# Two units for the modulated features, unit columns in the chunk's bank, and later steps around the halves of q, k and v

## The chip, the core and the metric

One core of a Trainium2 chip. The metric is the device time of one execution in microseconds. TensorE (PE) multiplies matrices into PSUM, which has eight banks; VectorE (DVE), ScalarE (ACT) and GpSimd (POOL) do elementwise work; SyncE (SP) issues nearly all DMAs, in the order in which they stand in the program. Each engine works through its own instructions in order and waits on the others by semaphores.

## What is computed

One layer of a hybrid mixer. 128 context tokens and 1024 latent tokens of 1024 features are normalised and modulated, projected by one matrix to q, k, v, an attention gate, an input of a recurrence and its gate; differential attention (8 heads, two softmax maps each) and a bidirectional gated recurrence run side by side, each output is multiplied by its SiLU gate, both go through one output projection, and the result is normalised, gated and added to x.

```python
sh, sc, gt = split(silu(cond) @ w_ada + b_ada)        # per token group
h = rms_norm(x, g_pre) * (1 + sc) + sh
q, k, v, g_att, x_lru, g_lru = split(h @ w_in)
o = softmax(q1 k1) v - lam * softmax(q2 k2) v          # per head, rotary q and k
att = rms_norm(o) * 0.8 * silu(g_att)
u = conv4(x_lru); a, b = gates(u)                      # both directions
lru = (scan(a_f, b_f) + reverse_scan(a_b, b_b)) * silu(g_lru)
y = x + gt * rms_norm(concat(att, lru) @ w_out)
```

Returned are y of both groups, the context's k and v, and the recurrence's final states.

## The kernel before

All 1152 tokens lie along the free axis, features along the partitions: `hTh[k]`, `hTl[k]` are the high and low fp16 halves of slice k (128 of 1024 features) of h. A weight of 48 (`order`, 128 output features each) is loaded as fp32 (`wraw`), its sum of squares taken on ACT (`w_square`, L286), summed over partitions by a matmul with ones (`w_unit`, L292) into one PSUM column, turned into a power of two on DVE (`power_of_two`, L190 to L195), scaled and cast to halves (`w_hi` on ACT, L306; `w_lo` on DVE, L312). `w_back` keeps the inverse of weight unit times feature unit. A projection chunk (`chunk`) is 24 matmuls: 8 slices by three products of halves, for 384 tokens, in one bank. `w_ahead` keeps three to five weights prepared ahead of the chunk in work.

PSUM is two pools: `big` (three banks, one buffer) and `small` (five banks). Chunks, unit columns (`wu`) and the small sums all take `small` buffers; a buffer is given out again in the order of release, and its next writer waits for its last reader.

**Stage 1, to 78 us.** Four parts of the modulation, A and C (scale) and B and D (shift) of the first and second half of the features, are products of `w_ada` (16 loads of 512 KB) with two columns. A, B and C are fp32 matmuls (`mod`, L419, 16 records each); D is summed on DVE (`mod_add`, L430 and L432, into `dsum`) and put across partitions by four matmuls. Squares of x are taken on ACT (`sqsum`), added on DVE (L499), summed by matmuls (`ssq`, L524), the root by `newton`, spread over partitions into `rb` (L530). Then `normed` (x times the root, L476), one unit for all features (`unit_h`), `modulate` on ACT or DVE, `h_lo` on DVE, and the first block's three chunks (x of block 0), slice by slice.

**Stage 2, to 415 us: eight rounds** of the recurrence. Round n: three chunks of the LRU gate (`g`), in rounds 1 to 6 three chunks of an attention gate (`ga` with hTh operands), then the four block gates of round n (`ga` in the `big` buffer, with `uh`, `ul`, `gwh`) with the three chunks of the next block's input (`x`) between them. `silu` (L703, ACT) and `silu_mult` (L709, DVE) read the gate chunks. DVE and ACT do round n-1's decays, weights, scans and mix meanwhile; `conv`, `split_u` make `u`, `uh`, `ul` of round n.

**Stage 3, to 760 us:** q, k chunks (24 matmuls each) and v tiles (24 matmuls of 256 columns), each followed by a `tick()`. `after(d, f)` runs f behind the d-th next tick. Steps of a q or k are `squares` (ACT, L868), `turned` (`power`, a matmul L879 and DVE, then `rope`, DVE), `halves` (ACT L893, DVE L894), `send` (DMA). Of a pair of v: `peak` (transpose L964, DVE), `spread` (L974), `halves` (ACT L983, DVE L984), `send` (L990). The output gate (`gate_step`) is summed on DVE and totalled by matmuls (`gacc`, L1031) of its halves (`ghl`). After the last v pair come two attention-gate blocks (`g_block`), six ticks, and attention's first loads (`load_k`, `load_q`, `load_wo`, `load_lt`) on SP.

**Stage 4:** attention and the output projection.

## Time and profile before

| | |
|---|---|
| median of 3 runs | 1281.56 us (1280.08 to 1284.37) |
| the profiled execution | 1290.48 us |
| its span | 1288.7 us |
| granted TensorE clock, mean | 0.963 of 2.4 GHz |
| TensorE busy | 1149.6 us (89%) |
| DVE busy | 1029.9 us (80%) |
| ACT busy | 781.9 us (61%) |
| POOL busy | 301.2 us (23%) |

The profile comes from one execution; its times are microseconds from the span's start, a mean time of an instruction is given in ns where that is said. A matmul's row shows its latency; matmuls overlap, so the distance of two starts is what one costs. "Idle" in brackets is how long the engine stood before the row, and what it waited for last. Two levels of the clock occur, 1.2 and 2.4 GHz; over a stretch the profile gives the mean as a share of 2.4.

### The profile page before, as it was taken

How to read it: one execution, taken by the hardware profiler on the slowest of the kernel's cores; microseconds unless marked ns; L12 is line 12 of the kernel's file. 1: busy time of each engine (PE TensorE's matmuls, PEld its weight loads, DVE VectorE, ACT ScalarE, POOL GpSimd, SP SyncE). 2: the span in 40 equal slices, each digit the busy share in tenths (PEclk: the TensorE clock that was granted, in tenths of full speed). 3: DMA queues.
4: the chain of work that ended last, by engine and by line, in shares of the span. 5: the costliest groups of instructions: out<-in, count | busy, mean ns of one | idle time of the engine just before them, and what ended most of it. 6: DMA issues, size and time to landing. Idle time of an engine off the chain costs nothing.

```text
span 1288.7 us, 20513 instructions
## 1 busy us (share of the span) xinstructions
PE 1149.6 (89%) x7792; PEld 792.3 (61%) x7792; DVE 1029.9 (80%) x1788; ACT 781.9 (61%) x1283; POOL 301.2 (23%) x172
## 2 busy tenths in 40 slices
PE   6599999999999679989999979988898888999787
PEld 1265655665666556675675847766666665667676
DVE  5886797779779767876867647898898989999877
ACT  4477467557746546544454347777777776777632
POOL 0000000000000000000000013345865576666624
PEclk8799999999999989999999999999999998999999
DMA  9321222231231243643525275899998889799864
GB/s 365 127 66 42 88 77 62 88 113 41 86 99 60 94 126 127 161 126 115 152 88 136 52 249 113 190 204 225 180 233 181 208 212 189 189 210 220 199 204 163
DMA packets 277818, 188.75 MB, mean 146 GB/s; under 512 B 196172, under 2 KB 246092, under 8 KB 276952
## 3 DMA queue, kind: packets, MB, share of 16 engines
q1 hardware_dynamic: 277432, 186.60, 54.4%
q8 instruction: 61, 1.00, 0.3%
q10 hardware_dynamic: 288, 0.85, 0.2%
q14 instruction: 37, 0.30, 0.1%
HBM read 102.20 MB, written 46.94 MB: 116 GB/s over the span
## 4 chain that ended last, share of the span: by engine, by line
PE 40%; DVE 32%; ACT 11%; DMA 7%; issue 6%; POOL 2%; SPq 2%; DVEq 0%; ACTq 0%; POOLq 0%
DVE mx L1195 6%; DVE e L1223 4%; PE ga L119 3%; DMA t<-a 3%; PE ga L120 3%; PE ga L121 2%; PE x L119 2%; PE x L120 2%; PE x L121 2%; PE s L1186 2%; DVE wlo L312 2%; PE s L1188 2%; PE v L119 2%; PE v L120 2%; PE v L121 2%
## 5 line engine op out<-in xcount | busy, mean ns | idle before, releaser
L1205 ACT ACTIVATE e<-s,mx,back 128x1152 f32<-128x1152 f32 (+1 forms) x144 | 175.5, 1219 | 70.7 <-DVE fa L1213 20.3
L1227 POOL TENSOR_TENSOR a<-e,a 128x1152 f16<-128x1152 f32 (+1 forms) x72 | 157.9, 2192 | 172.6 <-ACT a L1226 164.2
L113 POOL TENSOR_TENSOR wol<-wor,woh 128x512 fp32r<-128x512 f32 x24 | 33.5, 1398 | 694.1 <-ACT woh L218 694.0
L1195 DVE TENSOR_REDUCE mx<-s 128x1 f32<-128x1152 f32 (+1 forms) x144 | 177.3, 1232 | 22.7 <-PE s L1188 21.9
L120 PEld LDWEIGHTS <-whi 128*128 128x128 f16 x960 | 95.2, 99 | 82.3 <-issue 26.4
L119 PEld LDWEIGHTS <-whi 128*128 128x128 f16 x960 | 97.5, 102 | 66.3 <-issue 10.5
L121 PEld LDWEIGHTS <-wlo 128*128 128x128 f16 x960 | 95.2, 99 | 66.3 <-issue 5.6
L1186 PE MATMUL s<-kt,qt 128*128 128x384 f16 (+1 forms) x400 | 90.6, 332 | 46.2 <-ACT e L1205 42.9
L1223 DVE SCALAR_TENSOR_TENSOR e<-e,fa,e 128x1152 f32<-128x1152 f32 (+1 forms) x72 | 114.9, 1596 | 6.4
L119 PE MATMUL pv<-vt,t 128*128 128x128 f16 x584 | 104.7, 223 | 6.0 <-DMA t<-a 3.6
L119 PE MATMUL po<-woh,lt 128*128 128x512 f32 x216 | 98.8, 457 | 6.3 <-DVE acc L1152 3.3
L120 PE MATMUL pv<-vt,t 128*128 128x128 f16 x584 | 104.2, 222 | 0.0
L121 PE MATMUL pv<-vt,t 128*128 128x128 f16 x584 | 104.1, 222 | 0.0
L1226 ACT CAST a<-e 128x1152 f16<-128x1152 f32 (+1 forms) x72 | 75.8, 1053 | 40.7 <-DVE e L1223 25.9
L1188 PE MATMUL s<-kt,qt 128*128 128x384 f16 (+1 forms) x400 | 89.9, 331 | 0.0
L121 PE MATMUL po<-woh,lt 128*128 128x512 f32 x216 | 86.2, 399 | 0.0
L120 PE MATMUL po<-wol,lt 128*128 128x512 f32 x216 | 86.0, 398 | 0.0
L119 PE MATMUL v<-whi,hTh 128*128 128x256 f16 x288 | 80.1, 278 | 3.1 <-ACT qfq L735 2.6
L312 DVE SCALAR_TENSOR_TENSOR wlo<-wraw,wunit,whi 128x1024 f16<-128x1024 f32 x48 | 61.5, 1281 | 25.2 <-ACT whi L306 25.2
L120 PE MATMUL v<-wlo,hTh 128*128 128x256 f16 x288 | 80.1, 278 | 1.1 <-DVE wlo L312 1.1
L1186 PEld LDWEIGHTS <-qt 128*128 128x128 f16 x400 | 34.2, 99 | 76.0 <-issue 63.4
L121 PE MATMUL v<-whi,hTl 128*128 128x256 f16 x288 | 80.2, 278 | 0.0
(342 smaller groups left out, 3239.2 us busy)
## 6 DMA issues: line engine op xcount, KB each, us to landing
wraw<-in_w_in_dram SPq DMA_DIRECT2D x48, 512.0 KB, 3.6
lt<-mix SPq DMA_DIRECT2D x27, 512.0 KB, 4.5
qs<-hlq SPq DMA_DIRECT2D x64, 144.0 KB, 3.2
qt<-qs SPq DMA_DIRECT2D x72, 128.0 KB, 3.7
wa<-in_w_ada_dram SPq DMA_DIRECT2D x16, 512.0 KB, 11.0
wor<-in_w_out_dram SPq DMA_DIRECT2D x32, 256.0 KB, 3.3
mix<-amo SPq DMA_DIRECT2D x6, 1152.0 KB, 6.0
vs<-v SPq DMA_DIRECT2D x8, 640.0 KB, 6.3
```

The lines of the kernel that those rows point to most:

```text
L113: eng.tensor_tensor(out=lo, in0=val, in1=f(hi), op=ALU.subtract)
L119: PE.matmul(out, lhsT=lh, rhs=rh, start=start, stop=False)
L120: PE.matmul(out, lhsT=lh, rhs=rl, start=False, stop=False)
L121: PE.matmul(out, lhsT=ll, rhs=rh, start=False, stop=stop)
L312: V.scalar_tensor_tensor(out=lo[:, i % 2], in0=raws[i], scalar=wunit[:, i:i + 1], in1=hi[:, i % 2], op0=ALU.mult, op1=ALU.subtract)
L1186: PE.matmul(sps[:, j, :w_], lhsT=qt[:, mp], rhs=kt_[:, mp, c], start=True, stop=False)
L1188: PE.matmul(sps[:, j, :w_], lhsT=qt[:, 2 + mp], rhs=kt_[:, mp, c], start=False, stop=True)
L1195: V.tensor_reduce(out=d["mx"][:, mp:mp + 1], in_=sv, axis=AX.XY, op=ALU.max, negate=True)
L1205: S.activation(out=e_[:, :nk].rearrange("p (j c) -> p j c", c=w_), in_=sv, func=AF.Exp, bias=d["mx"][:, mp:mp + 1], scale=unit, accum_out= ...
L1223: V.scalar_tensor_tensor(out=e1, in0=e1, scalar=d["fa"], in1=e0, op0=ALU.mult, op1=ALU.subtract)
L1226: S.copy(out=a16[:, 0:nk], in_=e1)
L1227: G.tensor_tensor(out=a16[:, nk:2 * nk], in0=e1, in1=a16[:, 0:nk], op=ALU.subtract)
```

## The change

The features' unit becomes one per half (`unit_h(half)`, `uh` has two columns). `shares` works out the smaller of the two (`low`) and each half's share; a weight's first and second four slices are scaled by its unit times that half's share (`wboth`), so `w_hi` and `w_lo` are two instructions each, and `w_back` has one more. The first block has its weight scaled by the weight's unit alone; its slices 0 to 3 sum in the three `small` banks, slices 4 to 7 in the `big` buffer, and `x_first` adds the two, each times its own inverse. So slices 0 to 3 are modulated and multiplied ahead of the second half's scales. The loads of stage 1 are reordered (x ahead of most of `w_ada`), D goes through TensorE as A to C do (`mod_add`, `mod_total` and `dsum` are gone), and the order of all steps there is new. In the rounds of the recurrence the unit column of the next weight is written to column 400 and up of the first chunk's own bank, not into a `small` buffer of its own. In stage 3 `power` becomes a step of its own behind `rope`, a tick later (for q0 and q1 the squares are a tick earlier); v's `peak`, `spread`, `halves` and `send` are a tick later each; of the output gate, the totals are a tick or more behind their halves and `bias` a tick later.

```diff
         def w_back(i):
-            V.tensor_tensor(out=winv[:, i:i + 1], in0=wunit[:, i:i + 1], in1=uh[:, 0:1], op=ALU.mult)
+            V.tensor_scalar(out=wboth[:, i], in0=share, scalar1=wunit[:, i:i + 1], scalar2=None, op0=ALU.mult)
+            V.tensor_tensor(out=winv[:, i:i + 1], in0=wunit[:, i:i + 1], in1=low, op=ALU.mult)
             V.reciprocal(out=winv[:, i:i + 1], in_=winv[:, i:i + 1])
 
         def w_hi():
             i = cnt["cast"]
             if i % 2 == 0:
                 wts[i // 2] = tuple(wp.tile([P, 2, KT, P], F16, tag=t, name=f"{t}{i // 2}") for t in ("whi", "wlo"))
-            S.activation(out=wts[i // 2][0][:, i % 2], in_=raws[i], func=AF.Copy, scale=wunit[:, i:i + 1])
+            for x in range(2) if i else ():
+                r = slice(4 * x, 4 * x + 4)
+                S.activation(out=wts[i // 2][0][:, i % 2, r], in_=raws[i][:, r], func=AF.Copy, scale=wboth[:, i, x:x + 1])
+            if i == 0:
+                S.activation(out=wts[0][0][:, 0], in_=raws[0], func=AF.Copy, scale=wunit[:, 0:1])
             cnt["cast"] += 1
             return i
 
         def w_lo(i):
             hi, lo = wts[i // 2]
-            V.scalar_tensor_tensor(out=lo[:, i % 2], in0=raws[i], scalar=wunit[:, i:i + 1], in1=hi[:, i % 2], op0=ALU.mult,
-                                   op1=ALU.subtract)
+            for x in range(2) if i else ():
+                r = slice(4 * x, 4 * x + 4)
+                V.scalar_tensor_tensor(out=lo[:, i % 2, r], in0=raws[i][:, r], scalar=wboth[:, i, x:x + 1],
+                                       in1=hi[:, i % 2, r], op0=ALU.mult, op1=ALU.subtract)
+            if i == 0:
+                V.scalar_tensor_tensor(out=lo[:, 0], in0=raws[0], scalar=wunit[:, 0:1], in1=hi[:, 0], op0=ALU.mult,
+                                       op1=ALU.subtract)
...
-        def w_next(pair, m):
-            w_ahead(place[pair, m])
+        def w_next(pair, m, bank=None):
+            w_ahead(place[pair, m], bank)
...
-            for x in "A0 A1 w A2 A3 D0 B0 x0 D1 x1 B1 x2 x3 B2 x4 x5 B3 x6 C0 x7 D2 C1 D3 C2 C3 w w w".split():
+            for x in "A0 A1 w A2 A3 B0 B1 x0 x1 x2 x3 x4 x5 x6 x7 B2 B3 C0 C1 C2 C3 D0 D1 D2 D3 w w w".split():
...
-            def unit_h():
-                for half in range(2):
-                    PE.matmul(ssq[:, 40:41], lhsT=onesf, rhs=hsq[:, half:half + 1], start=half == 0, stop=half == 1)
-                power_of_two(uh[:, 0:1], ssq[:, 40:41])
+            def unit_h(half):
+                k0 = half * 4
+                PE.matmul(ssq[:, 40 + half:41 + half], lhsT=onesf, rhs=hsq[:, half:half + 1], start=True, stop=True)
+                power_of_two(uh[:, half:half + 1], ssq[:, 40 + half:41 + half])
                 for x in (sc1, sh1):
-                    V.tensor_scalar(out=x, in0=x, scalar1=uh[:, 0:1], scalar2=None, op0=ALU.mult)
+                    V.tensor_scalar(out=x[:, :, k0:k0 + 4], in0=x[:, :, k0:k0 + 4], scalar1=uh[:, half:half + 1], scalar2=None,
+                                    op0=ALU.mult)
+
+            def shares():
+                V.tensor_tensor(out=low, in0=uh[:, 0:1], in1=uh[:, 1:2], op=ALU.min)
+                V.reciprocal(out=share, in_=uh)
+                V.tensor_scalar(out=first_inv, in0=share, scalar1=1.0, scalar2=None, op0=ALU.mult)
+                V.tensor_scalar(out=share, in0=share, scalar1=low, scalar2=None, op0=ALU.mult)
+                V.reciprocal(out=winv[:, 0:1], in_=wunit[:, 0:1])
+                V.tensor_scalar(out=first_inv, in0=first_inv, scalar1=winv[:, 0:1], scalar2=None, op0=ALU.mult)
...
             w_lo(w_hi())
-            mod_rows(*A)
-            mod_turn(*A)
-            mod_add(*D_, 0)
-            for b in range(4):
+            for b in range(2):
                 mod(*B, b)
-            mod(*C, 0)
             for k in range(KT):
                 sqsum(k)
-                if k == 0:
-                    mod_add(*D_, 1)
-                if k == 5:
-                    mod_rows(*B)
-            mod_turn(*B)
-            scales(0)
-            bounds(0)
-            mod_add(*D_, 2)
+                if k == 2:
+                    mod_rows(*A)
+            mod_turn(*A)
             for t in range(NT):
                 PE.matmul(ssq[:, t:t + 1], lhsT=qsum[:, t * P:(t + 1) * P], rhs=onesf[:, 0:1], start=True, stop=True)
             V.tensor_scalar(out=xc, in0=ssq[:, :NT], scalar1=-0.5 / D, scalar2=-0.5 * EPS, op0=ALU.mult, op1=ALU.add)
             for k in NEWTON:
                 newton(k, xc, yc, tcol)
-            mod(*C, 1)
+            for b in range(2, 4):
+                mod(*B, b)
+            mod_rows(*B)
             for t in range(NT):
                 PE.matmul(rb[:, t // 3, (t % 3) * P:(t % 3 + 1) * P], lhsT=yc[:, t:t + 1].to_broadcast([P, P]), rhs=ident,
                           start=True, stop=True)
-            mod_add(*D_, 3)
+            mod_turn(*B)
+            normed(0)
+            scales(0)
+            bounds(0)
+            unit_h(0)
+            for b in range(2):
+                mod(*C, b)
+            normed(1)
+            modulate(0, S)
+            modulate(1, S)
+            normed(2)
+            h_lo(0)
+            normed(3)
+            for b in range(2, 4):
+                mod(*C, b)
+            modulate(2, S)
+            mod_rows(*C)
+            modulate(3, S)
+            h_lo(1)
+            normed(4)
+            mod_turn(*C)
+            for b in range(4):
+                mod(*D_, b)
+            mod_rows(*D_)
+            h_lo(2)
+            normed(5)
+            h_lo(3)
+            normed(6)
+            normed(7)
             w_square()
-            w_square()
-            mod(*C, 2)
-            w_unit(ssq)
-            for k in range(4):
-                normed(k)
-            mod(*C, 3)
-            mod_total(*D_)
-            mod_rows(*C)
-            mod_rows(*D_)
-            mod_turn(*C)
+            accs = [small(f"x0_{j}") for j in range(NCH)]
+            accb = big("x0b")
+
+            def first_chunk(k):
+                for j in range(NCH):
+                    chunk(accs[j] if k < 4 else accb[:, j], 16, 0, j, [k], k % 4 == 0, k % 4 == 3)
+
+            for k in range(2):
+                first_chunk(k)
             mod_turn(*D_)
             scales(1)
             bounds(1)
-            unit_h()
+            unit_h(1)
+            shares()
+            for k in range(2, 4):
+                first_chunk(k)
             w_unit(ssq)
-            for k in range(4, KT):
-                normed(k)
+            w_square()
+            modulate(4, S)
+            modulate(6, hi=V)
+            h_lo(6)
+            w_back(1)
+            h_lo(4)
+            modulate(5, S)
             one = w_hi()
-            accs = [small(f"x0_{j}") for j in range(NCH)]
-            ks_ = [0, 1, 7, 2, 3, 4, 5, 6]
-            modulate(0, hi=V)
-            h_lo(0)
-            for k in range(1, 7):
-                modulate(k, S)
-            for i in range(3):
-                w_back(i)
-            h_lo(1)
             modulate(7, hi=V)
             h_lo(7)
-            for k in range(2, 6):
-                h_lo(k)
+            h_lo(5)
             w_lo(one)
-            h_lo(6)
+            for x, k in enumerate((4, 6, 7, 5)):
+                for j in range(NCH):
+                    chunk(accb[:, j], 16, 0, j, [k], x == 0, x == 3)
+            w_back(w_unit(ssq))
             w_square()
-            for x, k in enumerate(ks_):
-                for j in range(NCH):
-                    chunk(accs[j], 16, 0, j, [k], x == 0, x == KT - 1)
             w_ahead(0, ssq)
...
                 acc = small(f"x{n + 1}_{j}")
                 chunk(acc, 16 + (n + 1) // 2, (n + 1) % 2, j)
                 if j == 0:
-                    w_next(16 + (n + 1) // 2, (n + 1) % 2)
+                    w_next(16 + (n + 1) // 2, (n + 1) % 2, acc)
...
+        def x_first():
+            for o, b, c in ((1, 0, CTX), (131, CTX, T)):
+                for j in range(NCH):
+                    lo_, hi_ = max(b, j * CH), min(c, (j + 1) * CH)
+                    if lo_ < hi_:
+                        dst, r = xp[0][:, o + lo_ - b:o + hi_ - b], slice(lo_ - j * CH, hi_ - j * CH)
+                        S.activation(out=dst, in_=accs[j][:, r], func=AF.Copy, scale=first_inv[:, 0:1])
+                        V.scalar_tensor_tensor(out=dst, in0=accb[:, j, r], scalar=first_inv[:, 1:2], in1=dst, op0=ALU.mult,
+                                               op1=ALU.add)
+
         load_gw(0)
-        for j in range(NCH):
-            x_evac(0, j, accs[j])
+        x_first()
...
-                    w_next(20 + n // 2, n % 2)
+                    w_next(20 + n // 2, n % 2, acc)
...
-                        w_next(12 + h // 2, h % 2)
+                        w_next(12 + h // 2, h % 2, acc)
...
             def turned():
-                power()
                 rope(t_, name)
...
-            steps = [squares, turned, halves, send]
+            steps = [squares, turned, power, halves, send]
...
-                for x, step in zip((1, 3, 4), steps[1:]):
+                for x, step in zip((1, 2, 3, 4), steps[1:]):
                     after(x, step)
             else:
 
-                for x, step in zip(((7, 8, 10, 11), (8, 10, 12, 13))[h], steps):
+                for x, step in zip(((6, 8, 9, 10, 11), (7, 10, 11, 12, 13))[h], steps):
                     after(x - 3 * h, step)
...
-            after(1, peak)
-            after(2, spread)
-            after(3, halves)
-            after(4, send)
+            after(2, peak)
+            after(3, spread)
+            after(4, halves)
+            after(5, send)
...
-                for w in range(2):
-                    after(3 + 2 * w, lambda w=w: split(w))
-                    after(4 + 2 * w, lambda w=w: total(w))
-                after(7, bias)
+                after(3, lambda: split(0))
+                after(5, lambda: (total(0), split(1)))
+                after(7, lambda: total(1))
```

## Rows read from the trace of the kernel before

**Rows 1.** The page: busy time, share of the span and instructions of TensorE.
```profile
PE 1149.6 (89%) x7792; PEld 792.3 (61%) x7792; DVE 1029.9 (80%) x1788; ACT 781.9 (61%) x1283; POOL 301.2 (23%) x172
```

**Rows 2.** TensorE's waits, 78 to 415 us: total us, times, longest.
```profile
PE ga L119 <- DVE lsg L709: 13.8, 6, 2.3
```

**Rows 3.** Timeline of round 1, 122 to 142 us: start, us, engine, line, operation.
```profile
124.48 0.15 DVE L190 TENSOR_SCALAR wunit<-wu 128x1 f32<-128x1 f32 x1
...
126.76 1.66 DVE L709 SCALAR_TENSOR_TENSOR lsg<-g,winv,lsg 128x384 f32<-128x384 f32 x3
...
127.43 0.48 PE L119 MATMUL ga<-hTh,whi 128*128 128x384 f16 x1 [2.30 <-DVE lsg L709]
...
128.02 0.52 PE L121 MATMUL ga<-hTh,wlo 128*128 128x384 f16 x1
...
130.56 0.33 PE L120 MATMUL ga<-hTl,whi 128*128 128x384 f16 x1
```

**Rows 4.** Busy time by stretch, two rounds: PE, PEld, DVE, ACT, POOL, granted clock, DMA.
```profile
157.00:203.50 46.50, 44.07 (x260) 28.37 (x258) 36.99 (x53) 28.77 (x34) 0.00 (x0) 0.96 0.24 78
203.50:248.30 44.80, 42.36 (x260) 27.81 (x258) 36.79 (x53) 28.75 (x34) 0.00 (x0) 1.00 0.25 82
```

**Rows 5.** Timeline of TensorE, 415 to 745 us, rows behind a wait.
```profile
453.90 0.59 PE L879 MATMUL unq<-sqq,onesf 128*128 128x1 f32 x2 [9.73 <-ACT jq L868]
...
474.98 0.27 PE L964 MATMUL vmt<-ident,vm 128*2 128x128 f32 x1 [3.96 <-ACT wjunk L286]
...
553.32 0.38 PE L879 MATMUL unk<-sqk,onesf 128*128 128x1 f32 x2 [4.23 <-ACT jk L868]
...
603.82 0.40 PE L1031 MATMUL gacc<-ghl,pick 128*2 128x512 f32 x1 [2.37 <-DVE ghl L113]
...
634.75 0.38 PE L879 MATMUL unk<-sqk,onesf 128*128 128x1 f32 x2 [1.28 <-ACT jk L868]
```

**Rows 6.** Timeline of ACT and DVE, 452 to 475 us.
```profile
452.60 1.16 ACT L868 ACTIVATE jq<-qfq 128x1152 f32<-128x1152 f32 x1 [10.50 <-DMA mix<-lmh]
...
474.66 0.17 DVE L957 TENSOR_REDUCE vm<-vmx 128x2 f32<-128x20 f32 x1
```

**Rows 7.** Timeline of DVE and of SP's queue, 745 to 752 us.
```profile
745.47 3.01 DVE L984 SCALAR_TENSOR_TENSOR v<-vf,sgv,v 128x1280 f16<-128x1280 f32 x2 [1.28 <-ACT v L983]
...
748.62 1.67 DVE L709 SCALAR_TENSOR_TENSOR sg<-ga,winv,sg 128x384 f32<-128x384 f32 x3
...
750.72 1.36 SPq L225 DMA_DIRECT2D kt<-ks  x2
```

**Rows 8.** Timeline of stage 1 and of the first round, to 91 us.
```profile
23.57 7.21 DVE L499 TENSOR_TENSOR qsum<-qsum,sq 128x1152 f32<-128x1152 f32 x5
...
34.97 4.00 PE L524 MATMUL ssq<-onesf,qsum 128*128 128x1 f32 x18 [1.91 <-DVE modT L448]
...
35.59 2.73 DVE L432 SCALAR_TENSOR_TENSOR dsum<-wa,cs,dsum 128x512 f32<-128x512 f32 x4
...
38.90 3.29 PE L419 MATMUL modpA<-wa,cs 128*2 128x512 f32 x4
...
44.33 1.88 PE L419 MATMUL modpA<-wa,cs 128*2 128x512 f32 x4
...
55.53 1.62 ACT L485 ACTIVATE xt<-xt,sh,sc 128x128 f32<-128x128 f32 x2 [3.83 <-DVE sh L473]
...
68.19 6.43 DVE L116 TENSOR_TENSOR hTl<-xt,hTh 128x1152 f16<-128x1152 f32 x5
...
78.58 0.32 PE L119 MATMUL g<-hTh,whi 128*128 128x384 f16 x1
...
79.79 0.88 DVE L619 TENSOR_SCALAR u<-xp,vec 128x1158 f32<-128x1158 f32 x1
...
86.28 1.37 DVE L113 TENSOR_TENSOR ul<-u,uh 128x1158 fp32r<-128x1158 f32 x1 [0.62 <-ACT uh L625]
...
90.28 0.47 PE L119 MATMUL ga<-uh,gwh 128*128 128x386 f32 x1
```

## What the change was predicted to do

> **What bounds the kernel now.** I read the page first: TensorE is busy for 1149.6 of 1288.7 us [rows 1], so an edit is worth what it takes out of TensorE's idle time, or what it adds to it. The change touches nothing behind the last projection, so I then took TensorE's waits stage by stage. In the recurrence (78 to 415 us) one wait stands out: 13.8 us in six pieces, the gate projection waiting for DVE's L709 [rows 2]. The timeline shows one piece: the second chunk of the attention gate starts at 127.43 after 2.30 us of idling, when L709 has freed a bank, and until 130.5 its matmuls follow each other at 0.32 us, then at 0.16 (1.2 against 2.4 GHz) [rows 3]. A round takes 46.5 us where the clock falls after the wait (granted 0.96 over the round; three of the six rounds) and 44.8 where it does not (1.00) [rows 4]. In the projections of q, k and v (415 to 745) the waits are 9.7 us for the squares of q0, 4.0 for the peak of v, 4.2 and 1.3 for squares of k, and twice 2.4 for the halves of the output gate [rows 5] (the twin of the 603.82 row is at 696.41); behind the five above two us I count the tail that [rows 4] shows, 1.6 each. Ahead of 78 us DVE and latencies lead: TensorE ends the first block only at 78.58 [rows 8].
>
> **(a) Recurrence: the unit column in the chunk's bank.** A round with an attention gate takes 12 buffers of the five `small` ones now: nine chunks and three unit columns. The second gate chunk therefore gets the bank of the first LRU-gate chunk, freed by L709. Without the columns a round takes nine, and the bank of L709 falls to the third gate chunk, 24 matmuls (3.9 us) later. TensorE would want it at 125.1 + 3.9 = 129.0; it is freed at the first third of L709, about 127.3 [rows 3]. New work ahead of L709 in that chain: a cast to low halves in two pieces of 512 columns (0.68 each against 1.28: +0.1) and one more small DVE operation (+0.19): 127.6. So 1.3 us of margin, and the wait goes. Worth: 6 x 2.3 = 13.8, and in three rounds the tail of 46.5 - 44.8, near 1.65: **-18.7 us**. TensorE is otherwise unbroken in these rounds, and DVE has 37 us of work in one [rows 4], so it does not take over at 42.5. Ends: -12 (tails stay) to -20.
>
> **(b) q, k, v: later steps.** Total of the output gate a tick after its halves are written: both waits of 2.37 and their tails of 1.6 go, **-7.9**. Power of k one tick later: at 553.32 TensorE first does 24 more matmuls of v (256 columns against 384: 3.9 x 2 / 3 = 2.6 us), so 4.23 becomes 1.6; with half a tail **-3.4**. The 1.28 at 634.75 goes, and five of its kind of about 0.3: **-2.6**. The pair 453.90 / 474.98 [rows 5] I cost at **0**: squares of q0 wait on ACT for the DMA of the last LRU mix until 452.60 [rows 6] whatever the tick, and DVE then works without a gap to the maximum of v at 474.66 [rows 6]. TensorE gets a further v tile and k chunk done meanwhile (-6.5), but the second squares now stand ahead of the v copies on ACT (1.3), four weights cost DVE 0.3 each more, and the second half-split now waits for a power that comes behind the rotation (1.4 + 1.0): the maximum lands near 479. Ends -4 and +4. Sum of (b): **-13.9**, ends -20 to -5.
>
> **(c) The step to attention.** v's halves and their DMAs move one tick. For the last pair this is past the last LRU-side block: the halves (two of 1.5 on DVE [rows 7]) now come behind the gate's L709 instead of ahead, and their DMAs behind the gate's, ahead of the first loads of attention on SP's queue. Those begin at 750.72, right behind L709 [rows 7]. L709 would end near 749.9, the second half 3.0 later, the issue of its DMA takes 0.7 (as each of the two there): loads begin at 753.6, **+2.9**. Nothing covers it: the first weights of the output projection wait for these loads. Ends 0 and +5.
>
> **(d) The first block.** Step by step, against the rows of [rows 8]. The loads put x in front of five 512 KB pieces, and DVE loses sixteen `dsum` operations of 0.68. Seven adds at 1.44 (7.21 / 5), begun at about 18.9 behind the first low half, end at 29.0; ssq started at 34.97 and now starts at 29.1. ssq 4.0, then B's second half on TensorE, 8 matmuls (0.82 each at 1.2 GHz by 3.29 / 4, 0.44 after that by 1.88 / 4; two at the one and six at the other give 4), then rb 2.2: it ends at 39.2 (before, by the matmuls behind it, 44.33). Turn, one normed slice (1.28), scales, bounds, unit, power: 4.4, an estimate (16 small DVE operations such as 124.48's 0.15, 0.19 with the step to the next, and three passes through TensorE). ACT begins to modulate at 43.6, not 55.53: 12 earlier. But now C and D both go through TensorE, 32 fp32 matmuls, behind the first unit: C from 42.4 to 51.4 (four us at 1.2 GHz, the rest at 0.44), its rows and turn 1.3, D 7.0: 59.7. Two slices of the first block (18 x 0.163) stand ahead of D's turn, 62.7; the same small steps without a slice 2.9: the second half's scales are there at **65.6**. Before, all eight slices were done 23 us after the scales (55.53 to 78.58); now four slices are left. DVE: shares and power of the next weight 2.5, two slices modulated, rounded and split (2 x 3.2), two more splits (2 x 1.285 [rows 8]), unit of the weight 0.6, 0.5 of waiting for the unit's matmul: 78.2. The order of the matmuls is 4, 6, 7, 5, and the low half of 4 is ready at 73.8; 36 matmuls, four us of them at 0.32, take 7.7: the block ends at **81.6**, 3.0 later than now. Behind it stand three things that were done earlier before: the next weight's unit, casts and splits (4.3), another unit (1.3), and the sum of two banks (four DVE operations by L709's 0.56 per 384 columns, 1.9). From conv to the end of ul it took 79.79 to 87.65; so ul is ready at 97.0, while the gate chunks on TensorE end at 94.0. The first gate starts at 97.1 (90.28 before [rows 8]): +6.8, and a tail of 1.6 behind the 3 us wait: **+8.4**. Ends: +2 (clock stays up through C, no wait at the gate) and +15 (1.2 GHz through D and the last 36).
>
> Casts in two pieces cost ACT and DVE 0.1 to 0.3 for each of 47 weights; TensorE bounds where they lie, and the chains that count have them above.
>
> **Sum**, against the profiled execution's own 1290.48 us (span 1288.7): -18.7 - 13.9 + 2.9 + 8.4 = -21.3. It stands 8.9 over the median of the three runs, 1281.56; I take the difference over to that, 1260.3, rounded: **1260**.
>
> **A rule that speaks against (a).** In [rows 3] the unit that DVE reads at 124.48 (`wu`) and the chunk that L709 reads at 126.76 (`g`) have banks of their own. The Trainium skill ("PSUM — Partial Sum Buffer", Terms) says that no two engines may be in one bank and quadrant at once, reads against reads included. By that rule ACT's read of the chunk has to be kept apart from DVE's read of the unit in the same bank. No row here shows both. If it were so and DVE came late, L709 would come late; the rival on (a) has what that costs.
>
> **Rivals.**
> - *The wait of (a) comes back elsewhere.* ACT's first read of a chunk waits until DVE has read the unit. For it: DVE works 37 of 45 us in the rounds [rows 4]. Against: DVE reads the unit at 124.48, 2.3 ahead of L709 on its own queue [rows 3], and the margin is 1.3. If lost: 18.7 less, 1279, which cannot be told from no change.
> - *The waits of (b) move.* The five buffers fill up with unevacuated tiles, or DVE is later than I think; (b) gives nothing: 1274.
> - *The first block gains.* If C and D cost less than I lay out and the second half's scales are there by 60, the block ends at 76 and the wait at the gate goes: (d) is -5 and not +8.4: 1247. For it: modulating starts 12 us earlier. Against: C and D are 14 us of fp32 matmuls in one queue at the best.
> - *Slower than before: TensorE stays at 1.2 GHz from 33 us to the first gate.* The new order breaks its work at 40, 51 and 67 us. Price over (d): B and rb 3.1, C and D 10.7, slices 0 and 1 2.8, the last 36 matmuls 3.8, 72 gate matmuls at +0.157 less the wait that they cover 8.3: 28.7, which gives 1289. It decides once more than 21.3 of this is spent: the low level has to last into the gate chunks (20.4 are spent ahead of them). Against: in [rows 3] it was back at 130.5, three us after the wait, and by [rows 8] between 42 and 44 (0.82 a matmul, then 0.47).
>
> **How the numbers follow.** Chances: forecast 0.58 (its own range 1252 to 1268), first block gains 0.14, (b) gives nothing 0.13, (a) comes back 0.07, slower 0.05, several mishaps at once 0.03. The predicted time is the forecast's, 1260. The range leaves out some of the gain rival and of the last three: 1246 to 1277. Faster by over 0.3% (3.8 us, about what a measurement of this kernel tells from no change): the first three, 0.85. Within: 0.08. Slower: 0.07.
>
> **What would show it.** (a): in the waits between 80 and 420 no row of the gate projection on L709, rounds of 42.5 us, granted clock 1.00. (b): no `gacc` wait, one of 1.6 at the first k power, the pair near q0 and v still 11 to 14 together. (c): the first `kt` load three us further behind the L709 of the seventh attention gate. (d): C and D at 42 to 60, the first gate at 97, with a wait of 3 us. Wrong: TensorE still waiting six times for L709, or the first gate before 90.

## Result and profile after

The changed kernel takes 1273.15 us (median of five, 1270.27 to 1273.68) beside 1282.44 for the kernel before on the same chip: a ratio of 0.9917 [0.9894, 0.9940], 9.3 us less. On another chip (chip 3 in the table below) it was 1272.23 beside 1286.58: 0.9888 [0.9866, 0.9909], 14.4 less. I had forecast 21.3 less (1260). So the sign and the range held, and the size was too large.

The profiled execution took 1273.15 us, its own median; its span is 1271.4. The page, busy time, share of the span and instructions, answers [rows 1]:

```profile
PE 1145.8 (90%) x7804; PEld 791.4 (62%) x7804; DVE 1037.2 (82%) x1880; ACT 787.8 (62%) x1330; POOL 300.1 (24%) x172
```

TensorE does nearly the same work (7804 matmul records for 7792) and stands less. Its waits from 78 to 402 us (total us, times, longest) answer [rows 2], and one round (columns as in [rows 4]) answers those:

```profile
PE ga L119 <- ACT gs L682: 2.5, 7, 1.5
PE ga L120 <- DVE ul L113: 1.0, 1, 1.0
```
```profile
156.44:198.87 42.43, 42.26 (x259) 27.73 (x258) 37.60 (x59) 28.95 (x37) 0.00 (x0) 1.00 0.27 86
```

All six waits on L709 (now L733) are gone, and a round takes 42.43 us at clock 1.00. In the projections the timeline of TensorE, rows behind a wait, answers [rows 5]; the last row is the step to attention:

```profile
421.02 0.27 PE L119 MATMUL v<-whi,hTh 128*128 128x256 f16 x1 [3.39 <-ACT qfq L759]
...
438.82 0.58 PE L913 MATMUL unq<-sqq,onesf 128*128 128x1 f32 x2 [5.35 <-ACT jq L902]
...
462.14 0.37 PE L997 MATMUL vmt<-ident,vm 128*2 128x128 f32 x1 [5.26 <-DVE vm L990]
...
536.43 0.38 PE L913 MATMUL unk<-sqk,onesf 128*128 128x1 f32 x2 [2.03 <-ACT jk L902]
...
617.62 0.58 PE L913 MATMUL unk<-sqk,onesf 128*128 128x1 f32 x2 [4.32 <-ACT jk L902]
...
743.99 0.76 PE L119 MATMUL po<-woh,lt 128*128 128x512 f32 x1 [4.59 <-DMA lt<-mix]
```

The two `gacc` waits are gone, q0's and k3's are shorter, v's is longer (5.26 for 3.96), and k5's squares, 1.28 before, now cost 4.32. The 3.39 at 421.02 was 2.60 in the kernel before; my list of waits left that row out:

```profile
436.03 0.27 PE L119 MATMUL v<-whi,hTh 128*128 128x256 f16 x1 [2.60 <-ACT qfq L735]
```

Stage 1 answers [rows 8]:

```profile
28.89 4.00 PE L521 MATMUL ssq<-onesf,qsum 128*128 128x1 f32 x18 [8.30 <-DVE modT L445]
...
43.21 5.16 PE L433 MATMUL modpA<-wa,cs 128*2 128x512 f32 x8
...
53.57 6.60 PE L433 MATMUL modpB<-wa,cs 128*2 128x512 f32 x15
...
74.06 0.48 PE L120 MATMUL x0b<-hTl,whi 128*128 128x384 f16 x1 [4.32 <-DVE hTl L116]
...
82.07 0.32 PE L119 MATMUL g<-hTh,whi 128*128 128x384 f16 x1
...
94.20 0.44 PE L119 MATMUL ga<-uh,gwh 128*128 128x386 f32 x1
```

### The profile page after: what moved, and what is told of

Same layout as the page of the kernel before. It is cut to its first block, busy times and chain, and to the rows that moved or that the text cites. A ratio compares the mean times of both kernels' runs of the same rounds, so it can differ in the third digit from the quotient of the medians.

```text
span 1271.4 us, 20656 instructions
## 1 busy us (share of the span) xinstructions
PE 1145.8 (90%) x7804; PEld 791.4 (62%) x7804; DVE 1037.2 (82%) x1880; ACT 787.8 (62%) x1330; POOL 300.1 (24%) x172
## 4 chain that ended last, share of the span: by engine, by line
DVE 38%; PE 34%; ACT 12%; issue 6%; DMA 5%; POOL 3%; SPq 1%; DVEq 0%; ACTq 0%; POOLq 0%
DVE mx L1228 6%; DVE e L1256 4%; DVE wlo L323 2%; PE ga L119 2%; DMA t<-a 2%; PE ga L120 2%; PE s L1219 2%; PE ga L121 2%; PE s L1221 2%; POOL a L1260 2%; ACT e L1238 2%; PE v L119 2%; PE v L121 2%; PE v L120 2%; PE x L119 1%
## 5 line engine op out<-in xcount | busy, mean ns | idle before, releaser
L1228 DVE TENSOR_REDUCE mx<-s 128x1 f32<-128x1152 f32 (+1 forms) x144 | 177.3, 1231 | 22.1 <-PE s L1221 21.3
L119 PE MATMUL pv<-vt,t 128*128 128x128 f16 x584 | 103.5, 221 | 4.9 <-DMA t<-a 2.7
L120 PE MATMUL pv<-vt,t 128*128 128x128 f16 x584 | 103.0, 221 | 0.0
L121 PE MATMUL pv<-vt,t 128*128 128x128 f16 x584 | 102.9, 221 | 0.0
L323 DVE SCALAR_TENSOR_TENSOR wlo<-wraw,wboth,whi 128x512 f16<-128x512 f32 x94 | 66.3, 747 | 18.3 <-ACT whi L313 18.3
```

What stands on the lines that cost most here:

```text
L119: PE.matmul(out, lhsT=lh, rhs=rh, start=start, stop=False)
L120: PE.matmul(out, lhsT=lh, rhs=rl, start=False, stop=False)
L121: PE.matmul(out, lhsT=ll, rhs=rh, start=False, stop=stop)
L323: V.scalar_tensor_tensor(out=lo[:, i % 2, r], in0=raws[i][:, r], scalar=wboth[:, i, x:x + 1], in1=hi[:, i % 2, r], op0=ALU.mult, op1=ALU.s ...
L1228: V.tensor_reduce(out=d["mx"][:, mp:mp + 1], in_=sv, axis=AX.XY, op=ALU.max, negate=True)
```

## The experiments

The change was cut into its three parts, run alone and in pairs; then single edits were tried on the changed kernel and on the best pair. The first table gives what was timed: `bank` is the unit column in the chunk's bank, `steps` the later steps, `block` the two units with the new first block and the casts in two pieces. Kernels with the same number under "chip" ran beside the same runs of before (medians 1286.26 on chip 2, 1286.58 on chip 3 and 1284.85 on chip 4; the first result is from chip 1).

| kernel | chip | median us | ratio to before |
|---|---|---|---|
| bank_only | 2 | 1266.88 | 0.9857 [0.9838, 0.9875] |
| steps_only | 2 | 1285.16 | 0.9989 [0.9978, 0.9999] |
| block_only | 2 | 1289.55 | 1.0020 [1.0001, 1.0039] |
| after_again (all three) | 3 | 1272.23 | 0.9888 [0.9866, 0.9909] |
| bank_steps | 3 | 1263.94 | 0.9824 [0.9804, 0.9845] |
| bank_block | 3 | 1268.56 | 0.9863 [0.9841, 0.9884] |
| bank_gate | 3 | 1261.96 | 0.9808 [0.9787, 0.9829] |
| after_bias | 4 | 1266.34 | 0.9847 [0.9825, 0.9869] |
| after_v_early | 4 | 1267.08 | 0.9859 [0.9837, 0.9881] |
| bank_split | 4 | 1263.66 | 0.9831 [0.9808, 0.9855] |
| best | 4 | 1259.44 | 0.9799 [0.9776, 0.9822] |

The second table splits each profiled execution at rows of its trace: the start of the first block gate (with `uh` and `gwh`), the end of the last block gate, the end of the last attention-gate chunk, the start of the first scores behind a wait for `e` (the step to attention), the span's end. The last column adds up, in the projections, what the matmuls of a chunk spaced as at 1.2 GHz took over the spacing at 2.4 (the clock's tails behind waits), from the starts of neighbouring rows with no other matmul and no idle time between them.

| kernel | first gate | recurrence | projections | step | attention | span | tails |
|---|---|---|---|---|---|---|---|
| before | 90.28 | 324.05 | 345.17 | 10.50 | 518.70 | 1288.7 | 8.5 |
| before_again | 90.14 | 324.07 | 345.51 | 10.82 | 515.56 | 1286.1 | 8.5 |
| after | 94.20 | 306.17 | 338.65 | 14.00 | 518.38 | 1271.4 | 9.1 |
| after_again | 96.43 | 306.20 | 338.90 | 13.54 | 515.83 | 1270.9 | 9.6 |
| bank_only | 88.64 | 302.32 | 343.15 | 11.25 | 518.34 | 1263.7 | 8.4 |
| steps_only | 88.47 | 323.95 | 340.90 | 14.40 | 516.58 | 1284.3 | 9.1 |
| block_only | 95.29 | 328.42 | 338.21 | 10.56 | 516.02 | 1288.5 | 5.2 |
| bank_steps | 90.43 | 302.31 | 338.71 | 13.77 | 516.38 | 1261.6 | 8.7 |
| bank_block | 95.41 | 306.16 | 339.63 | 10.98 | 514.62 | 1266.8 | 6.4 |
| bank_gate | 90.38 | 302.33 | 342.78 | 10.95 | 516.16 | 1262.6 | 9.2 |
| after_bias | 96.28 | 306.17 | 335.61 | 13.53 | 514.31 | 1265.9 | 8.2 |
| after_v_early | 94.12 | 306.17 | 337.61 | 11.08 | 515.52 | 1264.5 | 7.4 |
| bank_split | 88.97 | 303.62 | 340.99 | 11.92 | 514.80 | 1260.3 | 6.6 |
| best | 90.82 | 302.34 | 336.03 | 11.92 | 519.09 | 1260.2 | 5.1 |

Read down a column: the recurrence of one code repeats within 0.1 us, the projections of one code to 0.4 and the step to 0.5, while the first gate of one code moves by 2.3 (88.47 to 90.82) and attention, the same in all fourteen, by 4.8. The first gate and attention carry most of what one execution differs from the next; the three columns between can be read as they stand, and tell finer than the medians, whose ratios are good to 0.2% (2.5 us).

**The kernel before, once more.** No edit.

> The kernel before, unchanged, for a second profile. Its first profiled execution was 1290.48 us, 8 over its median; the changed kernel's was at its median. Theory 1 (the first profile was a long one in a single place, or in the clock's tails): this one has a span near 1279 to 1283, the six waits of 2.3 us on L709 stand again, and the stage in which the two profiles differ by some 8 us can be named; the profiled gain of 17.3 us then shrinks to about 9. Theory 2 (a profiled execution of this kernel is always longer): a span near 1288 again.

It took 1287.92 us. Up to attention the two profiles agree within 0.4 us in every stage, the six waits of 2.3 among them. The 2.6 us between their spans lie in attention (3.1 less there). No stage of the first profile was an accident that the sum could have leaned on. Theory 2 is nearer: this kernel's executions lie at 1279.5 to 1291.0 on chip 2, median 1286.26, and the 1281.56 that I started from was low for it.

**The bank alone.** On the kernel before (at three calls of `w_next`):

```diff
-        def w_next(pair, m):
-            w_ahead(place[pair, m])
+        def w_next(pair, m, bank=None):
+            w_ahead(place[pair, m], bank)
...
-                    w_next(20 + n // 2, n % 2)
+                    w_next(20 + n // 2, n % 2, acc)
```

> Of the change only the unit column in the chunk's bank, in the rounds of the recurrence. By the sum of the prediction: six waits of 2.3 us and three clock tails of 1.65 go, -18.7 us (about 1263 against 1282). Rival 1 (the tails are not in every execution): -13.8 at the least, about 1268. Rival 2 (the wait moves on, into the projections of q, k and v or into the start of attention): between 0 and -10, with no row of the gate projection behind L709 but new waits behind 415 us.

0.9857 of before, 18.4 us less; in the recurrence 324.05 became 302.32, 21.7 less. One round by stretch, and TensorE's waits from 78 to 391 us:

```profile
149.27:191.28 42.01, 42.01 (x259) 27.80 (x258) 36.82 (x53) 28.55 (x34) 0.00 (x0) 1.00 0.27 87
```
```profile
PE ga L119 <- ACT gs L658: 1.3, 1, 1.3
```

TensorE is busy all through the round. The prediction's mechanism holds, and in this stage it gives 3 us more than I summed. The kernel before shows why, around one such wait in a round at clock 1.00:

```profile
217.15 0.33 PE L121 MATMUL ga<-hTh,wlo 128*128 128x384 f16 x1
217.61 0.35 PE L292 MATMUL wu<-wsq,onesf 128*128 128x1 f32 x2
220.26 0.32 PE L119 MATMUL ga<-hTh,whi 128*128 128x384 f16 x1 [2.30 <-DVE lsg L709]
```

From start to start that is 3.11 us, and unbroken it is 0.30 (0.16 for the matmul and 0.14 for the unit's, as at 185.30, 185.46 and 185.60 in the changed kernel): 2.81 is lost, not the 2.30 in the bracket. Six times 2.8 and three tails of 1.65 are 21.8.

**The later steps alone.** On the kernel before, the change's edits to these lists of steps:

```diff
-            steps = [squares, turned, halves, send]
+            steps = [squares, turned, power, halves, send]
...
-            after(1, peak)
+            after(2, peak)
...
-                after(7, bias)
+                after(8, bias)
```

> Of the change only the later steps of q, k, v and of the output gate. By the sum of the prediction: -13.9 + 2.9, about -11. By the trace of the changed kernel, where a new wait of 4.3 us stands ahead of the squares of k5 and the first attention scores come only 6 us earlier over this stretch: about -4, with the transition to attention 3.5 later in it. Rival (later steps give nothing, the waits move): 0 +- 2.

0.9989, 1.4 less. By stage the projections fall by 4.3 to 4.6 and the step to attention rises by 3.6 to 3.9, so that 0.4 to 1.0 is left of the two: the rival came. TensorE's rows behind `gacc` are gone, and two of the rows behind a wait are these, with the row of DVE that the second goes back to:

```profile
550.69 0.38 PE L879 MATMUL unk<-sqk,onesf 128*128 128x1 f32 x2 [2.43 <-ACT jk L868]
...
632.24 0.58 PE L879 MATMUL unk<-sqk,onesf 128*128 128x1 f32 x2 [4.66 <-ACT jk L868]
```
```profile
621.32 0.68 DVE L1038 TENSOR_TENSOR gb<-gacc,gb 2x512 f32<-2x512 f32 x1 [2.71 <-DMA gb<-in_b_gate_dram]
```

**The first block alone.** The changed kernel with all steps as before (the last diff turned round) and the unit columns in buffers of their own:

```diff
-                    w_next(20 + n // 2, n % 2, acc)
+                    w_next(20 + n // 2, n % 2)
```

> The changed kernel with the unit columns in buffers of their own and with the earlier steps: of the change only the two units of the features and the new order of the first block. By the sum of the prediction +8.4; by the trace of the changed kernel +5.1 at the first gate of round 0, so +5 at the end if nothing takes it up, a little more if the split casts cost something behind 90 us (in the waits on L709, which come later by 0.3 each: +1.8). Rival (the later start is hidden by what follows): 0 to +2.

1.0020, 2.6 more. The first gate comes 5.1 later, as expected, and the recurrence takes 4.4 longer, but the projections take 7 less: the rest of the sum was wrong in both directions. Of the 7, 3.3 are tails that are gone (8.5 to 5.2). What the casts in two pieces bring by themselves is looked at below (bank_split); no run takes the rest apart.

**All three, and the pairs.** Beside after_again (no edit), bank_steps is the kernel before with the first two diffs, bank_block the changed kernel with the second turned round.

> The changed kernel again, beside the others and beside runs of the kernel before on the same chip. The three parts measured alone were -18.4, -1.4 and +2.6 us (0.9857, 0.9989, 1.0020). If they add up, the changed kernel stands at 0.9866, 17 us below before. If two of them take from each other, it stands as first measured, at 0.9917, 10 to 11 below.

> The kernel before with the unit column in the chunk's bank and with the later steps, but with its own first block and one unit for all features. If the parts add up, 0.9846 (-20). Rival (the later steps cost something where the recurrence no longer waits): at or above bank alone, 0.986 to 0.988. Beside the changed kernel this run tells what the new first block and the casts in two pieces cost there: 5.6 at the first gate and 0.42 in each of six rounds by the traces, so it should be 5 to 8 us below it.

> The changed kernel with the earlier steps of q, k, v and of the output gate. If the later steps gain about 1 as they do alone: 1 to 2 us above the changed kernel. If they cost something beside the other two parts (the wait of 4.3 ahead of the squares of k5, and 3 at the step to attention): up to 4 us below it.

By the medians the parts add up to 0.9866, 17 us less; it is 14.4, and the interval still reaches 17.2. On the bank alone the later steps gain 4.2 us (0.9857 to 0.9824); with the new block they cost 3.2 (0.9863 to 0.9888). The intervals overlap in both pairs; side by side on chip 3 the executions of bank_block (1268.06 to 1270.70) and of the changed kernel (1269.40 to 1275.08) barely do. The stages say the same in smaller numbers: with the old block the steps take 4.4 out of the projections (343.15 to 338.71), with the new one 0.7 to 1.0 (339.63 to 338.65 and 338.90), and in both cases they add 2.5 to 3.0 to the step to attention. So they are worth -1.9 beside the old block and +2 beside the new. The new block, on bank and steps, costs 8.2 us by the medians (0.9824 to 0.9888) and by the stages 3.8 to 6.0 at the first gate and 3.9 in the recurrence.

**The bias loaded earlier.** In the changed kernel DVE, TensorE, SP and ACT read like this around 606 us:

```profile
603.98 0.16 DVE L305 RECIPROCAL winv<-winv 128x1 f32<-128x1 f32 x1
606.69 0.68 DVE L1072 TENSOR_TENSOR gb<-gacc,gb 2x512 f32<-2x512 f32 x1 [2.54 <-DMA gb<-in_b_gate_dram]
...
609.34 1.28 DVE L885 STREAM_SHUFFLE rsk<-qfk 128x1024 f32<-128x1024 f32 x1
...
613.06 1.22 DVE L888 TENSOR_TENSOR qfk<-qfk,rsk 128x1024 f32<-128x1024 f32 x1
```
```profile
594.07 0.76 PE L1064 MATMUL gacc<-ghl,pick 128*2 128x512 f32 x2
```
```profile
601.19 0.33 SPq L942 DMA_DIRECT2D qfk<-in_cache_kT_dram  x1
603.02 0.33 SPq L284 DMA_DIRECT2D wraw<-in_w_in_dram  x1
603.45 0.31 SPq L1070 DMA_DIRECT2D gb<-in_b_gate_dram  x1
```
```profile
614.95 1.36 ACT L926 ACTIVATE hlk<-qfk,qksc 128x1280 f16<-128x1280 f32 x1 [6.56 <-DMA qs<-hlq]
616.22 1.25 ACT L902 ACTIVATE jk<-qfk 128x1280 f32<-128x1280 f32 x1
```

The last total, at 594.07, has long freed the buffer that the load shares with the gate's halves. The load goes out at 603.45 because SP issues in order: it stood for DVE's halves of a q until 601.14 and for the cast that frees a weight's buffer (DVE's L323, 601.57 to 602.99) until 603.02. DVE reaches the bias at 604.1 and stands until 606.69; behind it queue the rotation of k4 and its power, then on ACT k4's halves (put down to a DMA, but they begin when DVE has the power) and the squares of k5, and TensorE waits for those until 617.62. One edit tests it:

```diff
-                b_ = lp.tile([2, 2, 512], F32, tag="gw", name=f"gb{half}", bufs=1)
...
-                after(3, lambda: split(0))
+                after(3, lambda: (bias_load(), split(0)))
```

`bias_load` fills a buffer of its own (`tag="gb"`), which it needs so early; the run moves the loads and parts the buffers at once.

> The changed kernel with one edit: the two loads of the output gate's bias go out five ticks earlier, into a buffer of their own. In the changed kernel DVE stands 2.54 us for them; the rotation and the power of k4 queue behind it, ACT's halves and squares behind those, and TensorE waits 4.3 for the squares of k5 and loses 2.4 more in its clock's tail. Theory 1 (that stand of DVE is the cause): the wait falls to about 1.7 and its tail goes, -4 to -5 against the changed kernel (about 1268 where that has 1272). Theory 2 (the power behind the rotation is the cause, 4 us later in DVE's queue): the wait stays above 3 and the time within 1.5 of the changed kernel's.

0.9847, where the changed kernel has 0.9888: 5.3 us less. The two rows, DVE's and TensorE's:

```profile
606.56 0.66 DVE L1074 TENSOR_TENSOR gb<-gacc,gb 2x512 f32<-2x512 f32 x1
```
```profile
617.47 0.38 PE L913 MATMUL unk<-sqk,onesf 128*128 128x1 f32 x2 [1.67 <-ACT jk L902]
```

The times look alike only because this execution's first gate came 2.1 later than in the first one of the changed kernel. The stand is gone, 4.32 and 4.25 of waiting (after, after_again) became 1.67, the tail fell from 2.5 to 1.7 (I had expected it to go), and the projections are 3.0 to 3.3 shorter. Theory 1 holds. What is left of the 5.3 shows in no stage but attention, which moves by that much by itself.

**v's steps at their old ticks, in the changed kernel.**

```diff
-            after(2, peak)
-            after(3, spread)
-            after(4, halves)
-            after(5, send)
+            after(1, peak)
+            after(2, spread)
+            after(3, halves)
+            after(4, send)
```

> The changed kernel with v's steps at their old ticks. Theory 1 (the step to attention costs the 2.9 us of the prediction's term c): the stretch from the first score of attention to the end is near 527.5 and not 530.5, as in the kernels with the earlier steps, and the wait ahead of the maximum of v falls from 5.1 to 3 or 4: -3 to -5. Rival (attention's length varies by itself by as much from one execution to the next): no difference, +-1.

0.9859, 3.7 less than the changed kernel's 0.9888, in intervals that overlap. Around the step to attention, first the changed kernel (DVE, SP), then this one (SP, TensorE):

```profile
727.52 1.66 DVE L733 SCALAR_TENSOR_TENSOR sg<-ga,winv,sg 128x384 f32<-128x384 f32 x3
729.10 3.01 DVE L1017 SCALAR_TENSOR_TENSOR v<-vf,sgv,v 128x1280 f16<-128x1280 f32 x2
...
732.13 0.32 SPq L1023 DMA_DIRECT2D vs<-v  x1
733.63 0.82 SPq L229 DMA_DIRECT2D kt<-ks  x2
```
```profile
729.12 1.31 SPq L229 DMA_DIRECT2D kt<-ks  x2
...
739.70 0.47 PE L119 MATMUL po<-woh,lt 128*128 128x512 f32 x1 [1.69 <-DMA lt<-mix]
```

The first `kt` load starts 4.45 behind the end of the gate's `sg` in the changed kernel (729.18), 0.4 behind it here (728.68), as in [rows 7], and the wait for `lt` is 1.69 against 4.59: 2.9. The step takes 11.08 and not 13.5 to 14.0, and the projections are 1.0 to 1.3 shorter. Theory 1's sign and size hold for the step. The wait for the maximum of v, which it had falling, went the other way, from 5.26 to 9.22: TensorE comes to that row a chunk earlier, and DVE has the maximum no sooner (462.12 here, 462.14 in the changed kernel). Its measure (from the first score to the end, 526.8) was a poor one, since attention's own changes are in it.

**Casts in two pieces, one unit.** Bank alone, with `w_hi` and `w_lo` in two instructions each:

```diff
-            S.activation(out=wts[i // 2][0][:, i % 2], in_=raws[i], func=AF.Copy, scale=wunit[:, i:i + 1])
+            for x in range(2):
+                r = slice(4 * x, 4 * x + 4)
+                S.activation(out=wts[i // 2][0][:, i % 2, r], in_=raws[i][:, r], func=AF.Copy, scale=wunit[:, i:i + 1])
```

> The kernel before with the unit column in the chunk's bank, and with the casts of every weight in two pieces, by one unit and one scale. It tells what the pieces cost by themselves. Theory 1 (in the rounds of the changed kernel it is the pieces on ACT and DVE that bring the 0.17 us wait on the gates' evacuation, 0.42 from matmul to matmul): rounds of 42.4 and not 42.0, +2.5, and -1.6 from the first tile of v, which gets its halves earlier: +1 against bank alone. Theory 2 (the extra operation for a weight's two scales, or the order that the first block leaves, brings it): rounds of 42.0 and -1.6.

0.9831; against the bank's 0.9857 the intervals overlap. By stage: the recurrence takes 1.3 more (rounds of 42.17), the projections 2.2 less. So the pieces bring 0.16 of the 0.42 us that a round of the changed kernel takes over 42.01; whether the other 0.26 is the extra operation for the two scales or something else of the new block, no run shows. In the projections the first tile of v waits 0.5 for its low half and not 1.05, and the halves of the output gate come a little earlier:

```profile
580.48 0.40 PE L1035 MATMUL gacc<-ghl,pick 128*2 128x512 f32 x1 [2.08 <-DVE ghl L113]
...
670.49 0.39 PE L1035 MATMUL gacc<-ghl,pick 128*2 128x512 f32 x1 [2.07 <-DVE ghl L113]
```

The first of the two has no tail behind it, the second 1.6; in block_only and bank_block both are 2.2 long and neither has one. So with the new block the two waits that the later totals take away cost 5.0 from start to start (4.4 in the brackets) and no tails, not 7.9. By this sum it is a good part of why the later steps gain so little there.

**The gate's totals alone, and the best of the parts.** Bank, with the later totals and the early bias; then the same with `power` and the squares of q0 and q1 as in the change. v's steps, first block and one unit stay as before. The edit of bank_gate on bank_only:

```diff
-                for w in range(2):
-                    after(3 + 2 * w, lambda w=w: split(w))
-                    after(4 + 2 * w, lambda w=w: total(w))
-                after(7, bias)
+                after(3, lambda: (bias_load(), split(0)))
+                after(5, lambda: (total(0), split(1)))
+                after(7, lambda: total(1))
+                after(8, bias)
```

> The kernel before with the unit column in the chunk's bank, and of the later steps only the output gate's: its totals two ticks behind their halves, its bias a tick later, and the two loads of the bias five ticks earlier, into a buffer of their own. In the changed kernel DVE stood 2.54 us for these loads with the rotation and the power of k4 queued behind, and TensorE then waited 4.3 for the squares of k5. If that is where the gain of the later totals went, here both waits of 2.4 on the halves go with their clock tails and no wait of over 2 comes in their place: -6 to -8 against bank alone (1259 to 1261 where that has 1267). Rival (the next wait stands right behind whatever is done): -1 to -3.

> The kernel before with the unit column in the chunk's bank, the power behind the rotation and the earlier squares of q0 and q1, the later totals of the output gate, and its bias loaded five ticks earlier; v's steps, the first block and the one unit stay as before. By the rows: against bank with all later steps (0.9824) the 3 us at the step to attention and the 4.5 ahead of the squares of k5 go, of which some 2 come back: 0.978 to 0.981, 1258 to 1262. Rival (a wait in the projections only moves to the next full buffer): 0.982 to 0.984.

bank_gate: 0.9808, but its projections are only 0.4 shorter than the bank's; the rest of the 6 us between the two medians shows in no stage of the profiled execution, which was the longest of its five. The median is near the one that I expected, the rows are the rival's, so I take the number for luck. The two waits went to the next full buffer, this one and its twin at 678.84, neither with a tail:

```profile
600.77 0.32 PE L119 MATMUL k<-hTh,whi 128*128 128x384 f16 x1 [2.04 <-DVE wunit L190]
```

With `power` later too (best) these are gone, and k5's squares cost 1.82, k3's 1.38, q0's 5.63; v's maximum is 8.33 late. The projections take 336.0, 7.1 less than the bank's, and the kernel 1259.44 us: 0.9799 [0.9776, 0.9822], as expected (0.978 to 0.981) and below the changed kernel. It has neither the new block nor v's later steps; what either would cost in it, no run shows.

## Why the prediction was right or wrong

The step that failed is (b), the later steps: forecast at -13.9, they took 0.7 to 1.0 out of the projections of the changed kernel. The other three terms came within about 3.

**(a), -18.7: right in mechanism, low by 3.** The waits and all three tails went; measured -21.7 in the recurrence. The term that was mis-sized is the price of a wait: I took the bracket (2.30), the rows lose 2.81 from start to start.

**(a)'s rival, the bank: it happened, and cost little.** I had the wait of ACT on DVE as a rival at 0.07. In the kernel before, with the column in a bank of its own, ACT reads the next input's chunk right behind the chunk's last matmul, ahead of DVE's read of the column at 234.06:

```profile
233.76 0.73 ACT L612 ACTIVATE xp<-x,winv 128x128 f32<-128x128 f32 x2 [0.61 <-PE x L121]
```

In the changed kernel (TensorE, DVE, ACT, one round):

```profile
185.46 0.28 PE L296 MATMUL x<-wsq,onesf 128*128 128x1 f32 x2
```
```profile
189.43 0.15 DVE L194 TENSOR_SCALAR wunit<-x 128x1 f32<-128x1 f32 x1
```
```profile
189.62 0.73 ACT L636 ACTIVATE xp<-x,winv 128x128 f32<-128x128 f32 x2 [4.39 <-DVE wunit L194]
190.24 1.23 ACT L682 ACTIVATE gs<-ga,vec 128x1158 f32<-128x1158 f32 x1
```
```profile
191.52 0.44 PE L119 MATMUL ga<-uh,gwh 128*128 128x386 f32 x1 [0.17 <-ACT gs L682]
```

ACT could read the chunk at 185.6 and reads it at 189.62, right behind DVE's look at one column of the same bank; the gates' evacuation queues behind on ACT, and TensorE stands 0.17 for it. The Trainium skill ("PSUM — Partial Sum Buffer", Terms) rules out two engines in one bank and quadrant at once, reads against reads included; these rows agree with that, since ACT waits here for DVE though both only read. What I had wrong is the place: I looked at the chunk that L709 reads, where DVE's own order covers it, and not at the next input's chunk, whose reader stands ahead of the gates. Of the 4.16 us from the column's matmul to ACT's read, bank_only has 3.50 (178.29 to 181.79), and there TensorE doesn't wait in these rounds (42.01 us each). With the casts in two pieces (bank_split) it is 0.16 a round, in the changed kernel 0.42.

**(b), -13.9: the step that failed.** With the old block it was worth -4.3 to -4.6 in the projections, with the new one -0.7 to -1.0. Three lines of it: the row of 1.28 at 634.75, which I let go to nothing, became 4.3 and a tail of 2.5; I moved the bias a tick later and never costed it, though it issues two DMAs behind all that SP still stands for, and DVE waits for them with the rotation in its queue (after_bias: 3.0 to 3.3 us in the projections, 5.3 by the medians). The tails: I took 1.6 off for each wait that went and half of that at k3, 4.0 in all, and the tails grew from 8.5 to 9.1, since the five waits of two us and more that came or stayed (3.39, 5.35, 5.26, 2.03, 4.32) each have theirs, 1.4 to 2.5. And `gacc`, -7.9, was counted in the kernel before; beside the new block its two waits have no tails (bank_block); the casts in two pieces alone take one of the two (bank_split). Right in it: k3's wait (2.03, I said 1.6), the pair at q0 and v (10.6 together, I said 11 to 14), both `gacc` rows gone. The rival "the waits of (b) move" at 0.13 is what came.

The projections still fell by 6.6, through two gains that the prediction doesn't have: the bank by itself took 2.2 off (345.3 to 343.15), the new block beside it 3.5 more (to 339.63). Counted in the other order, the later steps take 4.4 and the new block nothing behind them (338.71 against 338.65). So what one of the two takes is not there for the other; which waits they share is shown for `gacc` alone.

**(c), +2.9: right.** 4.59 against 1.70 is 2.9, and the queue is in the order that I wrote. The first `kt` load starts 4.0 further behind the gate's `sg` (4.45 against 0.43 in [rows 7]), not three, since SP also stands for the landing of v's halves, from 732.5 to 733.6. The step takes 13.5 to 14.4 in the five kernels with v's later steps and 10.5 to 11.9 in the nine without.

**(d), +8.4: near, by other parts.** In brackets what I had laid out: C ran from 43.2 to 51.8 (42.4 to 51.4), D from 53.6 to 60.6 (52.7 to 59.7), the second half's scales have their unit at 66.5 (65.6), the block ends at 82.07 and 84.3 (81.6). The first gate is 5.1 later, not 6.8: the wait there is 0.96 and has no tail, since `ul` was ready 1.5 earlier than I laid out. What I costed at nothing behind the first gate ("TensorE bounds where they lie", of the casts in two pieces) costs 0.42 in each of six rounds and 1.2 in round 0: 3.9 in the recurrence (306.17 against 302.32), of which the pieces alone bring 1.3 (bank_split). The two are 9.0, and on bank and steps the medians say 8.2.

**The base.** I carried a difference over from a profile at 1290.48 to a median of 1281.56. Beside the changed kernel the kernel before measured 1282.44 on chip 1 and 1286.58 on chip 3; the changed kernel 1273.15 and 1272.23. So 5 of the 12 us by which I missed the first difference are the kernel before being quicker in the first runs. That 1273 lies beside the 1274 of the rival that came is in part luck: the quicker base, the larger (a) and the gains in the projections that I didn't have largely cancel. By stages of the profiles (means of two) the change is worth +5.1, -17.9, -6.6, +3.1 and nothing in attention: -16.3, against my -21.3. Why the first chip ran the kernel before 2 to 4 us faster stays open; its five executions (1280.08 to 1286.51) lie inside the spread of chip 2, and no profile was taken of a quick one.

## What to carry to other kernels

Price a wait from start to start of the rows around it, not by its bracket, and give a step back its tail only when no other wait stays near it. When a step is moved by a tick, list its loads and ask what stands ahead of them in the queue that issues them, and which in-order engine will stand for them: here a bias of two rows held up a rotation, a power, two ACT passes and a chunk. And measure the parts of a change in pairs: by the stages the later steps gain with one first block and lose with another.

## What the runs showed of the hardware

A wait of 2.30 us left TensorE's clock at 2.4 GHz in three rounds and was followed by 1.65 us of tail in three others; two waits of 2.08 and 2.07 in one run did the same, one each way. The wait for q's copies ahead of the second v tile had no tail with 2.60 in the two profiles of the kernel before and with 3.26 in bank_split, and one of 1.4 with 2.60 in bank_only. So a tail can't be read off the length of one wait. The same rounds (1, 2 and 6) had the tail in all three profiles with the old waits and the old first block (before, before_again, steps_only). The recurrence and the projections of one code repeat to 0.1 and 0.4 us from one execution to the next; nearly all that executions differ by lies ahead of the first gate (2.3 us) and in attention (4.8 us).
